# A transformer block pair on one core: a delta rule without GpSimd, deferred transposes, shared raw buffers and single-step weight sums

## The chip, the cores and the metric

The kernel runs on one core of a Trainium2 chip. The core has TensorE (matrix products, "PE"), VectorE ("DVE"), ScalarE ("ACT"), GpSimd ("POOL") and SyncE ("SP", which here only issues DMA transfers). Each takes its instructions in the order in which they were written for it, and they wait for each other by semaphores. The metric is the device time of one execution in microseconds.

## The reference

Two blocks work on 512 tokens of width 1024, in float32. All of this is computed:

- Block one: `x + mixer(rmsnorm(x))`. The mixer projects to seven groups of columns; one half is a spatial gating in chunks of 128, the other a gated delta rule with 4 heads of 128 (state `S_t = exp(g)(I − beta k kᵀ) S_{t−1} + beta k vᵀ`, output `Sᵀq`, normalised and gated); both go through `w_out`. Then cross-attention on a memory of 256 rows (`xa_wq`, `xa_wk`, `xa_wv`, `xa_wo`), then `square(relu(h @ ffn_w1)) @ ffn_w2` with 4096 hidden columns.
- Block two: a mixer of an mLSTM (4 heads) and a sliding-window attention (16 heads), two gates, two branch products and `w_out_2`; an MLP of the same shape (`w_up`, `w_down`); a gated product with a per-layer embedding; a last norm.

## The kernel before

Activations lie with features on the partitions: 8 tiles of 128x512. To hold float32 precision every operand is split into a rounded part and a rest, and every product is three matmuls (`mm3`, L285–L287: hi·hi, hi·lo, lo·hi into one PSUM tile). A weight granule of 128x8x256 (512 KB) is loaded by SyncE into a raw buffer `wr` (L263), cast to `wh` by ScalarE (L266), and the rest `wl = wr − wh` is made by VectorE (L267). So each granule passes SyncE's queue, ScalarE's queue and VectorE's queue before TensorE can use it, and the next load needs a raw buffer that L267 has released.

The order of instructions on each engine is set by a scheduler over the written program, which also moves later products ahead to fill TensorE; `keep_in_program_order` and `issue_after` add edges that it must hold.

Stages by time: projections and spatial gating 0–75 us; delta rule 75–310; rest of `w_out` and cross-attention to 395; first MLP to 800; second mixer to 1180; gates, branches, `w_out_2` to 1340; second MLP to 1700; the last product to the end.

**Delta rule.** `dn_head` handles one head with 128x128 tiles, 4 at a time (one PSUM bank, tag `c0` or `c1` by the head's parity, two buffers each). It transposes q, k, v (L565), takes their norms (`rsqrt` by small integer and Newton steps, L180–L185, on VectorE), makes the decay mask `E` (`slg`: L594 on GpSimd, L571 on TensorE, exp L597 on ScalarE, mask L598 on GpSimd, scale L599 on VectorE), `ked`, `kdec`, `vt` (L601, L602, L610), `M` and `QKT` (L605, L608), three masked copies of `M` (L626, GpSimd), inverts the triangular part by 15 steps of L642/L644 and block products (L622–L682), and scans the chunks (L696 `dY`, L702 `dS`, L709 and L713 `do`). At the end `o` is multiplied with the gate (L727, GpSimd) and with its norm (L728, VectorE), transposed on TensorE (L731) and split (L317/L318) for `w_out`. TensorE fills a head's waits with other products: `do_qk`, `do_v` (projections of later heads), `do_wa` (`w_out`'s first half), and `memory()` (L768, the memory's k and v).

**MLPs.** The second product of each MLP is done by seven products in place of eight of half-size blocks. Besides blocks a11, a12, a21, a22 of a weight it needs four sums of them. `sum_jobs` makes sums in DRAM by DMA: copies issued by ScalarE (L217) and accumulating copies issued by GpSimd (L220). `job()` is called at each weight granule and, every third or second call, runs one step. For `ffn_w2` two of the four sums are made so, and the third and fourth by one VectorE addition of 128x1024 (L890) into a raw buffer of its own; `w_down_2` has all four made by DMA, 1 MB of copies and 1 MB of adds per step, all in the second mixer and after. `st_weights` loads them (L887), splits them (L314/L315); `st_gemm` runs the seven products into PSUM tiles X, Y, Z and adds them to the residual (L924). In the MLPs raw, hi and lo buffers rotate together: three sets, or two "x" sets, of which two and two raw.

**Second mixer.** L1187 (mLSTM mask on VectorE) feeds L1197; L1263/L1264 split a query for the attention's scores L1285. The gate granules `w_in_ga` are read between.

## Time and profile before

| | |
|---|---|
| time, median of 3 | 1746.3 us (1746.27 to 1752.83) |
| profiled execution | 1746.58 us, span 1744.8 us |
| busy in the span | PE 97%, DVE 70%, ACT 46%, POOL 8% |
| bytes by DMA | 226.62 MB, mean 130 GB/s |

Windows are stretches of the span: busy time of each engine in it, instructions in brackets, then the granted TensorE clock (1.00 is full), the mean busy share of the 16 DMA engines and GB/s. A row of waits has the engine, its line, what it waited for, total us, times, the longest. A timeline row has start and duration in us, engine, line, operation, tiles, and in square brackets how long the engine was idle before and what ended it. A group's row has count, busy us and mean ns.

### The profile page before, as it was taken

The page shows a single profiled execution, that of the slowest core. Times are in us where ns is not written, and L with a number is a line of the kernel's source. Part 1 is how long each engine was busy: PE and PEld are TensorE (multiplying, and loading weights), DVE is VectorE, ACT ScalarE, POOL GpSimd, SP SyncE. Part 2 cuts the span into 40 slices and gives each one's busy share as a digit, 9 for nine tenths or more (in the row PEclk, how much of TensorE's full clock was granted, in tenths as well). Part 3 has the DMA queues.
Part 4 walks back from the last instruction along what each step waited for, and adds up shares of the span by engine and source line. Part 5 has one row for each costly group of instructions (what it writes and reads, how often), then busy time and mean ns, then how long its engine had stood idle before and what let it go on. Part 6 is the DMA issues. An engine that isn't in the chain of part 4 may idle for free.

```text
span 1744.8 us, 26033 instructions
## 1 busy us (share of the span) xinstructions
PE 1694.7 (97%) x9924; PEld 1465.6 (84%) x9924; DVE 1222.6 (70%) x2532; ACT 800.3 (46%) x1386; POOL 137.6 (8%) x156
## 2 busy tenths in 40 slices
PE   9999999999999999999999999999999999999998
PEld 8987788777898989888888886777888888898987
DVE  6998886756686777679745568775566766666775
ACT  5344544444444343444444456653244444444553
POOL 2212111100101000000010201011100000000000
PEclk9999999999999999999999999999999999999999
DMA  6322244716648353324477845449772343444331
GB/s 198 98 74 63 66 119 117 169 60 184 155 134 216 98 175 111 131 85 120 103 164 175 182 98 101 118 111 232 159 204 79 127 151 118 147 128 141 115 121 49
DMA packets 88605, 226.62 MB, mean 130 GB/s; under 512 B 13600, under 2 KB 14752, under 8 KB 88480
## 3 DMA queue, kind: packets, MB, share of 16 engines
q1 hardware_dynamic: 60368, 173.48, 31.1%
q0 software_dynamic: 13824, 25.17, 10.4%
q10 hardware_dynamic: 14288, 26.30, 5.5%
q8 instruction: 78, 1.28, 0.3%
q14 instruction: 47, 0.39, 0.1%
HBM read 222.56 MB, written 52.43 MB: 158 GB/s over the span
## 4 chain that ended last, share of the span: by engine, by line
PE 77%; DVE 11%; DMA 6%; ACT 4%; issue 2%; SPq 0%; ACTq 0%; DVEq 0%
PE psd L286 19%; PE psd L287 19%; PE psd L285 19%; PE x L285 4%; PE x L286 3%; PE x L287 3%; DVE wl L267 2%; ACT wh L266 1%; DMA wr<-in_w_in_ga_dram 1%; PE c L622 1%; PE lg L1285 1%; DMA wr<-sums_ffn_w 1%; PE po L1312 1%; DVE e L372 1%; ACT wh L314 1%
## 5 line engine op out<-in xcount | busy, mean ns | idle before, releaser
L285 PE MATMUL psd<-S,wh 128*128 128x512 f32 (+1 forms) x1256 | 484.2, 386 | 2.6 <-DVE e L768 1.7
L287 PE MATMUL psd<-S,wl 128*128 128x512 f32 (+1 forms) x1256 | 484.8, 387 | 0.8 <-DVE wl L267 0.8
L286 PE MATMUL psd<-S,wh 128*128 128x512 f32 (+1 forms) x1192 | 458.8, 385 | 0.5 <-DVE S L315 0.5
L267 DVE TENSOR_TENSOR wl<-wr,wh 128x1024 fp32r<-128x1024 f32 (+3 forms) x190 | 229.8, 1210 | 144.9 <-ACT wh L266 143.8
L266 ACT CAST wh<-wr 128x1024 fp32r<-128x1024 f32 (+3 forms) x190 | 194.6, 1025 | 214.4 <-PE psd L286 93.0
L285 PEld LDWEIGHTS psd<-S,wh 128*128 128x128 f32 x1256 | 237.3, 189 | 48.7 <-DVE e L768 1.9
L287 PEld LDWEIGHTS psd<-S,wl 128*128 128x128 f32 x1256 | 236.6, 189 | 46.2 <-DVE wl L267 1.6
L286 PEld LDWEIGHTS psd<-S,wh 128*128 128x128 f32 x1192 | 225.2, 189 | 43.3 <-DVE S L315 1.2
L285 PE MATMUL psd<-wh,S 128*128 128x256 f32 (+2 forms) x480 | 136.1, 284 | 1.2 <-ACT S L1090 1.2
L286 PE MATMUL psd<-wl,S 128*128 128x256 f32 (+2 forms) x480 | 136.4, 284 | 0.7 <-DVE wl L267 0.7
L287 PE MATMUL psd<-wh,S 128*128 128x256 f32 (+2 forms) x480 | 136.1, 284 | 0.0
L285 PE MATMUL x<-S,wh 128*128 128x256 f32 x452 | 129.0, 287 | 3.5 <-DVE x_fm L924 2.5
L286 PE MATMUL x<-S,wh 128*128 128x256 f32 x452 | 126.6, 281 | 0.0
L287 PE MATMUL x<-S,wl 128*128 128x256 f32 x452 | 125.8, 281 | 0.0
L314 ACT CAST wh<-wr 128x1024 fp32r<-128x1024 f32 (+1 forms) x76 | 71.5, 942 | 118.4 <-PE psd L286 40.1
L924 DVE TENSOR_TENSOR x_fm<-x_fm,x 128x256 f32<-128x256 f32 x192 | 78.7, 418 | 45.8 <-PE x L287 45.3
L286 PE MATMUL psd<-S,whx 128*128 128x512 f32 (+1 forms) x296 | 108.5, 366 | 0.0
L285 PE MATMUL psd<-S,whx 128*128 128x512 f32 (+1 forms) x296 | 108.0, 366 | 0.0
L287 PE MATMUL psd<-S,wlx 128*128 128x512 f32 (+1 forms) x296 | 107.2, 362 | 0.0
L315 DVE TENSOR_TENSOR wl<-wr,wh 128x1024 fp32r<-128x1024 f32 (+1 forms) x76 | 82.7, 1090 | 28.3 <-ACT wh L314 27.5
L285 PE MATMUL x<-S,whx 128*128 128x256 f32 x316 | 91.5, 290 | 5.1 <-DVE x_fm L924 2.5
L285 PEld LDWEIGHTS psd<-wh,S 128*128 128x128 f32 x480 | 91.0, 190 | 1.8 <-ACT S L1090 1.4
(460 smaller groups left out, 3198.3 us busy)
## 6 DMA issues: line engine op xcount, KB each, us to landing
wr<-in_ffn_w_dram SPq DMA_DIRECT2D x30, 512.0 KB
wr<-in_w_up_dram SPq DMA_DIRECT2D x20, 512.0 KB
wrx<-in_ffn_w_dram SPq DMA_DIRECT2D x18, 512.0 KB
wr<-sums_w_down SPq DMA_DIRECT2D x18, 512.0 KB
wr<-in_w_in_qk_dram SPq DMA_DIRECT2D x16, 512.0 KB
sums_ffn_w<-in_ffn_w_dram ACTq DMA_DIRECT2D x32, 256.0 KB
sums_w_down<-in_w_down_dram ACTq DMA_DIRECT2D x16, 512.0 KB
sums_w_down<-in_w_down_dram ACTq DMA_DIRECT2D x32, 256.0 KB
```

What stands on the lines that cost most here:

```text
L266: nc.scalar.copy(hi[:, c], raw[:, c])
L267: nc.vector.tensor_tensor(out=lo[:, c], in0=raw[:, c], in1=hi[:, c].bitcast(F32), op=ALU.subtract)
L285: mm(ps, ah, bh, start=first, stop=False, skip_group_check=more)
L286: mm(ps, ah, bl, start=False, stop=False, skip_group_check=more)
L287: mm(ps, al, bh, start=False, stop=last, skip_group_check=more)
L314: nc.scalar.copy(hi, src)
L315: nc.vector.tensor_tensor(out=lo, in0=src, in1=hi.bitcast(F32), op=ALU.subtract)
L372: nc.vector.scalar_tensor_tensor(out=c[:, s:], in0=xr[:, :T - s], scalar=w(j), in1=c[:, s:], op0=ALU.mult, op1=ALU.add)
L622: nc.tensor.matmul(ps[:, b * n:(b + 1) * n], lhs[:, b], rhs(b), start=True, stop=True)
L924: TT(out=x[n][t], in0=x[n][t], in1=ps, op=op)
L1285: nc.tensor.matmul(ps[:, i, K0:], qs[:, 2 * e2 + i, cs], kd[:, w, kc], start=(w == 0), stop=(w == 1))
L1312: nc.tensor.matmul(po, vhl[:, kb, j], pT[:, w], start=(kk == kks[0] and w == 0), stop=(kk == 1 and w == 1))
```

## The change

1. In `dn_head` GpSimd does nothing more. `slg` is four ScalarE copies with a scale (L602 in the new numbering); mask and scale of `E` are four VectorE operations in place of one on each of two engines; `ked`, `kdec`, `vt` are four, three and four ScalarE copies (L609) in place of VectorE operations; masked copies, memsets and the gate (L736) go to VectorE; the scale by the norm goes to ScalarE (four times L738). The sum of squares in the mixer's norm goes from GpSimd to VectorE.
2. A head's last step (transposes, now L743, and split) is returned as `fin` and written later, behind the last matmul written by then. `do_wa` 0 to 3 and `do_qk(3)` stand before head 3, `memory()` is a generator whose eight granules are written around and after head 3.
3. In the MLPs raw buffers rotate by themselves, five in all, and the third and fourth sums are computed into a11/a12's own raw buffer.
4. Both MLPs have two sums made by DMA and two by VectorE. A job is one 256 KB copy or one 256 KB add; all jobs of both are queued during the first mixer, two are run per granule up to the first MLP, then one, and one more in each `st_gemm`.
5. The seven products come in another order (a12 second).

Three places of the order. The first is the end of head 1's solve on TensorE. `c_…` are PSUM tiles, dV, dS, dY and vt belong to head 1 here, dk and dq to head 2. Before:

```order
L676 MATMUL c_297_1768<-dT_1669,dM_1654 64x64 x4
L286 MATMUL psd_2733<-S_122_933,wh_2714 128x512
L287 MATMUL psd_2733<-S_121_932,wl_2715 128x512
L285 MATMUL psd_2733<-S_121_932,wh_2714 128x512
L681 MATMUL c_299_1775<-dV_1679,dA_298_1773 64x64 x4
```

and now (L676 and L681 are L685 and L690):

```order
L690 MATMUL c_298_1797<-dV_1701,dA_297_1795 64x64 x4
L578 MATMUL c_392_2248<-dk_1890 128x128 x3
L578 MATMUL c_299_1803<-vt_1660,dV_1701 128x128 x4
L578 MATMUL c_300_1809<-dV_1701,ked_1659 128x128 x4
L578 MATMUL c_394_2255<-dq_1889,dk_1890 128x128
L711 MATMUL c_302_1816<-vt_1660,kdec_1658 128x128
L578 MATMUL c_394_2255<-dq_1889,dk_1890 128x128 x3
L718 MATMUL c_304_1820<-vt_1660,QKT_1680 128x128
L705 MATMUL c_305_1823<-dS_303_1818,ked_1659 128x128
L572 MATMUL c_396_2262<-masks,dv_1973 128x128 x4
```

Head 2's products L578 into c_392 and c_394 stand among head 1's last steps, and large projections no longer part them. VectorE at the same place, now:

```order
L691 TENSOR_TENSOR dV_1701<-dV_1701,c_298_1797 64x4x64
L593 TENSOR_TENSOR ds_384_2216<-ds_384_2216,beta_1058 128x4
L597 TENSOR_TENSOR dvi_2221<-dss_2182,dry_2203 128x4
L730 TENSOR_SCALAR dsc_2444<-dry_2203 128x4
L595 TENSOR_TENSOR dkd_2219<-ds_384_2216,ee_1093 128x4
L607 SCALAR_TENSOR_TENSOR slg_2223<-slg_2223,ds_384_2216,masks 128x128 x4
L308 SCALAR_TENSOR_TENSOR S_459_2572<-e_464_2586,vec,S_458_2571 128x256
L614 TENSOR_TENSOR dM_2253<-c_392_2248,slg_2223 128x512
```

Head 2's L595 (dkd, which L609 needs for kdec) stands behind head 1's L691, which waits for L690; the copies of kdec release the PSUM buffer into which c_394 goes.

The second place is VectorE's end of head 3, from the second Newton step on. Before:

```order
L185 SCALAR_TENSOR_TENSOR doy_2690<-dot_2691,doy_2690 128x4
L318 SCALAR_TENSOR_TENSOR S_595_3188<-psd_3430,rsmy_2880,S_594_3187 128x256
L183 TENSOR_TENSOR dot_2691<-doy_2690 128x4
L267 TENSOR_TENSOR wl_3557<-wr_3555,wh_3556 128x1024
L184 SCALAR_TENSOR_TENSOR dot_2691<-dot_2691,dso_2678 128x4
```

and now:

```order
L184 SCALAR_TENSOR_TENSOR doy_3002<-dot_3003,doy_3002 128x4
L182 TENSOR_TENSOR dot_3003<-doy_3002 128x4
L183 SCALAR_TENSOR_TENSOR dot_3003<-dot_3003,dso_2990 128x4
L184 SCALAR_TENSOR_TENSOR doy_3002<-dot_3003,doy_3002 128x4
L735 TENSOR_TENSOR dsc_2996<-dsc_2996,doy_3002 128x4
```

The steps of other work between are gone. On TensorE, the matmuls between the head's last L713 (now L722) and its transposes were 28 of 256 and 17 of 512 columns and are now 15 of 512 columns.

The third place is GpSimd's queue of the `w_down` sums. Before:

```order
L220 DMA sums_w_down_2_81<-in_w_down_dram 128x512 x2
L220 DMA sums_w_down_1_80<-sums_w_down_1_80 128x512
L220 DMA sums_w_down_0_79<-sums_w_down_0_79 128x512
L220 DMA sums_w_down_3_82<-in_w_down_dram 128x512 x2
L220 DMA sums_w_down_2_81<-sums_w_down_2_81 128x512
```

and now:

```order
L222 DMA sums_w_down_0_79<-in_w_down_dram 128x512
L222 DMA sums_w_down_0_79<-sums_w_down_0_79 128x512
L222 DMA sums_w_down_1_80<-in_w_down_dram 128x512
L222 DMA sums_w_down_1_80<-sums_w_down_1_80 128x512
L222 DMA sums_w_down_2_81<-in_w_down_dram 128x512
```

Four adds per group became two, one in each job. The diff, cut to its core:

```diff
-        self.sums = {n: [self.dp.tile([P, m, T], F32, tag=f"{n}{g}", name=f"sums_{n}_{g}") for g in range(16)]
-                     for n, m in (("ffn_w2", 2), ("w_down_2", 4))}
-        self.jobs, self.calls, self.every = [], 0, 1
-        self.adder = tc.nc.gpsimd
+        self.sums = {n: [self.dp.tile([P, 2, T], F32, tag=f"{n}{g}", name=f"sums_{n}_{g}") for g in range(16)]
+                     for n in ("ffn_w2", "w_down_2")}
+        self.jobs, self.made, self.rate, self.rn = [], {}, 1, 0
...
-        full = S[0].shape[1] == 4
-        def copy(o, i):
-            self.tc.keep_in_program_order(nc.scalar.dma_start(o, i))
-        def add(o, i):
-            self.tc.keep_in_program_order(nc.gpsimd.dma_start(o, i, accum_op=ALU.add))
-        def step(i):
-            if i < n:
-                a, s = W[i], S[i]
-                copy(s[:, 1::2], a[:, 0:s.shape[1] // 2])
-                for j in range(0, s.shape[1], 2):
-                    copy(s[:, j:j + 1], a[:, 2:3])
-            if 0 <= i - 1 < n:
-                a, s = W[i - 1], S[i - 1]
-                add(s[:, 0:1], a[:, 3:4])
-                if full:
-                    add(s[:, 2:3], a[:, 0:1])
-            if 0 <= i - 2 < n:
-                s = S[i - 2]
-                add(s[:, 1:2], s[:, 0:1])
-            if full and 0 <= i - 3 < n:
-                s = S[i - 3]
-                add(s[:, 3:4], s[:, 1:2])
-        self.jobs += [(lambda i=i: step(i)) for i in range(n + 2 + full)]
+        self.made[name] = 0
+        def copy(i, j, k):
+            if 0 <= i < n:
+                with self.tc.issue_after(self.last_cast.ins):
+                    nc.scalar.dma_start(S[i][:, j:j + 1], W[i][:, k:k + 1])
+        def add(i, j, src):
+            if 0 <= i < n:
+                nc.gpsimd.dma_start(S[i][:, j:j + 1], src(i), accum_op=ALU.add)
+                self.made[name] += j
+        for i in range(n + 2):
+            self.jobs += [lambda i=i: copy(i, 0, 2), lambda i=i: add(i - 1, 0, lambda g: W[g][:, 3:4]),
+                          lambda i=i: copy(i, 1, 0), lambda i=i: add(i - 2, 1, lambda g: S[g][:, 0:1])]
     def job(self):
-        self.calls += 1
-        if self.jobs and self.calls % self.every == 0:
-            self.jobs.pop(0)()
+        for _ in range(self.rate):
+            if self.jobs:
+                self.jobs.pop(0)()
     def wtiles(self, kt, n):
-        p, b, x = self.wp, (2, 3), ""
+        p, b, x = self.wp, 3, ""
+        q, c, y = self.wp, 2, ""
         if self.wx is not None:
-            self.wn = (self.wn + 1) % 5
+            self.wn, self.rn = (self.wn + 1) % 5, (self.rn + 1) % 5
             if self.wn > 2:
-                p, b, x = self.wx, (2, 2), "x"
-        return (self.t(p, [P, kt, n], "wr" + x, bufs=b[0]), self.t(p, [P, kt, n], "wh" + x, F32R, bufs=b[1]),
-                self.t(p, [P, kt, n], "wl" + x, F32R, bufs=b[1]))
+                p, b, x = self.wx, 2, "x"
+            if self.rn > 1:
+                q, c, y = self.wx, 3, "x"
+        return (lambda: self.t(q, [P, kt, n], "wr" + y, bufs=c), lambda: self.t(p, [P, kt, n], "wh" + x, F32R, bufs=b),
+                lambda: self.t(p, [P, kt, n], "wl" + x, F32R, bufs=b))
...
-            eng = self.adder if k < KT - 1 else nc.vector
-            eng.tensor_tensor(out=acc, in0=acc, in1=sq, op=ALU.add)
+            nc.vector.tensor_tensor(out=acc, in0=acc, in1=sq, op=ALU.add)
...
-            self.dn_head(h, *qk[h], v[h], pr, gate, yb_h, yb_l)
+            fins.append(self.dn_head(h, *qk[h], v[h], pr, gate, yb_h, yb_l))
...
         do_head(1)
         do_qk(2)
         do_v(2)
-        do_head(2)
         do_wa(0)
         do_qk(3)
+        self.behind(fins[0])
+        do_head(2)
+        for g in (1, 2, 3):
+            do_wa(g)
+        self.sum_jobs("ffn_w2")
+        self.sum_jobs("w_down_2")
+        self.rate = 2
+        next(mem)
+        self.behind(fins[1])
         do_head(3)
-        do_wa(1)
-        do_wa(2)
-        do_wa(3)
+        for _ in range(5):
+            next(mem)
+        self.behind(fins[2])
+        next(mem)
+        next(mem)
+        fins[3]()
         self.yb = ([yb_h[:, k] for k in range(4)], [yb_l[:, k] for k in range(4)])
+    def behind(self, f):
+        with self.tc.issue_after(self.last_mm.ins):
+            f()
...
-        nc.gpsimd.tensor_tensor(out=slg, in0=self.maskb("slower"), in1=pr["g"][:, :, h:h + 1].broadcast_to([P, NB, P]), op=ALU.mult)
+        for b in range(NB):
+            nc.scalar.activation(slg[:, b], self.mask("slower"), AF.Copy, scale=pr["g"][:, b, h:h + 1])
         psD = mm4(lambda b: slg[:, b], lambda b: self.mask("upper"))
         E = slg
         nc.scalar.activation(E, v4(psD), AF.Exp)
-        nc.gpsimd.tensor_tensor(out=E, in0=E, in1=self.maskb("upper"), op=ALU.mult)
-        TT(out=E, in0=E, in1=col(s1), op=ALU.mult)
+        for b in range(NB):
+            V.scalar_tensor_tensor(out=E[:, b], in0=E[:, b], scalar=s1[:, b:b + 1], in1=self.mask("upper"), op0=ALU.mult, op1=ALU.mult)
         kdec, ked, vt = b4("kdec"), b4("ked"), b4("vt")
-        TT(out=ked, in0=v4(psk), in1=ed.broadcast_to([P, NB, P]), op=ALU.mult)
-        TT(out=kdec[:, :NB - 1], in0=v4(psk)[:, :NB - 1], in1=col(kd)[:, :NB - 1], op=ALU.mult)
+        scaled = lambda out, ps, f, n=NB: [nc.scalar.activation(out[:, b], blk(ps, b), AF.Copy, scale=f(b)) for b in range(n)]
+        scaled(ked, psk, lambda b: ed[:, b])
+        scaled(kdec, psk, lambda b: kd[:, b:b + 1], NB - 1)
...
-        TT(out=vt, in0=v4(psv), in1=col(ri), op=ALU.mult)
+        scaled(vt, psv, lambda b: ri[:, b:b + 1])
...
-            nc.gpsimd.tensor_tensor(out=out, in0=M, in1=self.maskb(n), op=ALU.mult)
+            TT(out=out, in0=M, in1=self.maskb(n), op=ALU.mult)
...
-        nc.gpsimd.memset(Tb, 0.0)
-        nc.gpsimd.memset(flat(Tb)[:, 0::17], 1.0)
+        V.memset(Tb, 0.0)
+        V.memset(flat(Tb)[:, 0::17], 1.0)
...
-        nc.gpsimd.tensor_tensor(out=o, in0=o, in1=gate[:, :, h * P:(h + 1) * P], op=ALU.mult)
-        TT(out=o, in0=o, in1=col(sc), op=ALU.mult)
-        psy = psc()
+        TT(out=o, in0=o, in1=gate[:, :, h * P:(h + 1) * P], op=ALU.mult)
         for b in range(NB):
-            nc.tensor.transpose(blk(psy, b), o[:, b], ident)
-        self.split_sb(yb_h[:, h], yb_l[:, h], psy, self.vec[:, C_ONORM:C_ONORM + 1])
+            nc.scalar.activation(o[:, b], o[:, b], AF.Copy, scale=sc[:, b:b + 1])
+        def fin():
+            psy = psc()
+            for b in range(NB):
+                nc.tensor.transpose(blk(psy, b), o[:, b], ident)
+            self.split_sb(yb_h[:, h], yb_l[:, h], psy, self.vec[:, C_ONORM:C_ONORM + 1])
+        return fin
...
+        while self.made[name] <= g:
+            self.jobs.pop(0)()
...
+        def parts_of(raw):
+            rn = self.rn
+            _, hi, lo = self.wtiles(2, T)
+            self.rn = rn
+            return raw, hi(), lo()
+        def load(*srcs):
+            raw, hi, lo = (f() for f in self.wtiles(2, T))
             j = 0
             for src in srcs:
                 m = src.shape[1]
                 nc.sync.dma_start(raw[:, j:j + m], src)
                 j += m
-            if not srcs:
-                nc.vector.tensor_tensor(out=raw, in0=ra, in1=rb, op=ALU.add)
-            c = slice(first, first + n)
+            return raw, hi, lo
+        def split(raw, hi, lo, c=slice(0, 2)):
             self.split_sb(hi[:, c], lo[:, c], raw[:, c])
-            out.extend((hi[:, i], lo[:, i]) for i in range(first, first + n))
-            return raw
-        ra = part([a[:, 0:2]])
-        if s.shape[1] == 4:
-            part([s[:, 0:2]])
-            part([s[:, 2:4]])
-            part([a[:, 3:4]], 1)
-            return [out[i] for i in (0, 2, 3, 1, 4, 5, 6)]
-        part([s[:, 0:1], a[:, 3:4]])
-        rb = part([a[:, 2:3], s[:, 1:2]], 1, 1)
-        part([])
-        return [out[i] for i in (0, 2, 4, 1, 5, 6, 3)]
+            return [(hi[:, i], lo[:, i]) for i in range(c.start, c.stop)]
+        A = load(a[:, 0:2])
+        a11, a12 = split(*A)
+        B = load(a[:, 2:3], s[:, 1:2])
+        s2, = split(*B, slice(1, 2))
+        C = load(s[:, 0:1], a[:, 3:4])
+        nc.vector.tensor_tensor(out=A[0], in0=A[0], in1=B[0], op=ALU.add)
+        s1, a22 = split(*C)
+        s3, s4 = split(*parts_of(A[0]))
+        return a11, a12, s2, s1, s3, s4, a22
...
         w = self.st_weights(name, g)
+        self.job()
...
-        prod(1, Z, 4, True)
-        add(1, 1, Z, ALU.subtract)
+        prod(1, Y, 1, True)
+        add(0, 0, Y)
         prod(2, X, 5, False)
         add(0, 1, X)
-        prod(3, Y, 1, True)
-        add(0, 0, Y)
+        prod(3, Z, 4, True)
+        add(1, 1, Z, ALU.subtract)
...
-        K.mixer()
-        K.adder = K.nc.vector
-        K.sum_jobs("ffn_w2")
-        K.every = 3
-        mem = K.memory()
+        mem = K.mixer()
...
-        K.every = 1
+        K.rate = 1
...
-        K.sum_jobs("w_down_2")
-        K.every = 2
```

20 lines of the change are left out of this document (11 added, 9 removed).

## The prediction

> **What bounds the kernel now.** I read busy time by stage first, then the waits of TensorE in each stage, the granted clock around the longest of them, and last the instructions there.
>
> ```profile
> core 0: us, PE busy (x) PEld busy (x) DVE busy (x) ACT busy (x) POOL busy (x), PEclk, DMA share, GB/s
> 425.00:450.00 25.00, 25.00 (x109) 20.29 (x108) 12.91 (x16) 8.98 (x12) 4.14 (x5) 1.00 0.66 166
> 75.00:310.00 235.00, 222.42 (x1473) 195.47 (x1472) 199.18 (x535) 107.77 (x261) 37.55 (x33) 0.99 0.32 93
> 400.00:800.00 400.00, 393.43 (x2333) 345.81 (x2332) 288.42 (x454) 181.05 (x245) 17.33 (x21) 1.00 0.49 141
> 800.00:1180.00 380.00, 364.67 (x2130) 310.33 (x2129) 260.00 (x715) 192.53 (x411) 37.67 (x45) 0.98 0.56 131
> 1340.00:1700.00 360.00, 356.30 (x2179) 315.29 (x2178) 250.66 (x412) 165.89 (x228) 0.00 (x0) 1.00 0.40 129
> ```
>
> TensorE bounds it. Where it runs without a gap (109 matmuls of 512 columns in 25 us, 229 ns each) nothing can be had, and the change keeps the number of matmuls. What can move is the time in which TensorE is idle, length less busy time: 12.6 us in the delta rule (75–310), 6.6 in the first MLP (400–800), 15.3 in the second mixer (800–1180), 3.7 in the second MLP (1340–1700). The waits of these four stretches, in that order:
>
> ```profile
> PE c L731 <- DVE do L728: 6.6, 4, 2.4
> PE c L571 <- DVE kdec L602: 1.8, 2, 1.1
> PE psd L285 <- DVE e L768: 1.7, 1, 1.7
> PE c L622 <- DVE dTb L648: 1.3, 2, 1.0
> ...
> PE x L285 <- ACT whx L314: 3.3, 3, 2.2
> PE x L285 <- DVE x_fm L924: 2.1, 4, 0.9
> ...
> PE lg L1285 <- DVE qs L1264: 5.0, 3, 4.2
> PE m L1197 <- DVE E L1187: 3.1, 1, 3.1
> ...
> PE x L285 <- DVE x_fm L924: 3.0, 4, 1.4
> ```
>
> A long wait costs more than itself, since the granted clock falls behind it:
>
> ```profile
> 180.00:184.00 4.00, 3.63 (x16) 3.34 (x17) 3.96 (x8) 1.85 (x6) 0.00 (x0) 0.59 0.00 0
> 768.00:772.00 4.00, 4.00 (x23) 4.00 (x23) 2.75 (x4) 0.62 (x1) 0.00 (x0) 0.60 0.34 119
> 884.00:888.00 4.00, 2.90 (x14) 2.46 (x15) 4.00 (x10) 0.96 (x2) 3.30 (x4) 1.00 0.83 183
> 1096.00:1100.00 4.00, 0.21 (x1) 0.00 (x0) 1.52 (x2) 2.20 (x3) 0.00 (x0) 0.86 0.70 202
> 1100.00:1104.00 4.00, 3.55 (x14) 3.34 (x14) 3.46 (x8) 1.62 (x2) 0.00 (x0) 0.50 0.46 136
> 1104.00:1108.00 4.00, 4.00 (x19) 3.38 (x19) 2.58 (x18) 2.12 (x9) 0.00 (x0) 0.78 0.44 131
> ```
>
> Lost clock is (1 − PEclk) × 4 us: 1.6 behind the L731 wait at 180, 1.6 behind the whx wait, 3.4 (0.6 + 2.0 + 0.9) around the L1285 wait. Behind the L1197 wait at 885 nothing was lost, so it isn't certain.
>
> **Part 1, the engines of a delta head.** GpSimd's work goes away, and that matters through VectorE:
>
> ```profile
> 230.40 1.28 POOL L598 TENSOR_TENSOR slg<-slg,masks 128x512 f32<-128x512 f32 x1 [17.44 <-ACT slg L597]
> 232.19 1.26 POOL L626 TENSOR_TENSOR dA<-dM,masks 128x512 f32<-128x512 f32 x1 [0.51 <-DVE dry L185]
> 230.50 1.22 DVE L644 TENSOR_TENSOR dV<-dV,dA 32x28 f32<-32x28 f32 x1
> 232.23 1.24 DVE L183 TENSOR_TENSOR drt<-dry 128x8 f32<-128x8 f32 x1
> L648 DVE TENSOR_TENSOR dTb<-dY,masks 128x128 f32<-128x128 f32 x4 | 3.2, 796 | 0.2 <-DMA dY<-dV 0.2
> ```
>
> A VectorE operation that starts within a GpSimd one ends with it: 128x8 takes 1.24 us, 32x28 1.22. The 1.7 us wait for e L768 stands at 234.07, right behind these two holds, and dTb's 796 ns is such a hold as well (1.3 us of waits). I count both as gained, **+3.0**. The wait for kdec (1.8) I leave: its chain at 115 us is VectorE's square-root steps, which stay.
>
> What VectorE gets in return:
>
> ```profile
> L599 DVE TENSOR_TENSOR slg<-slg,ds 128x512 f32<-128x512 f32 x4 | 2.7, 683 | 0.0
> L707 DVE SCALAR_TENSOR_TENSOR dS<-dS,ee,c 128x128 f32<-128x128 f32 x8 | 2.8, 345 | 1.0 <-PE c L702 0.9
> L719 ACT ACTIVATE dA<-do 128x128 f32<-128x128 f32 x16 | 4.9, 308 | 5.2 <-DVE do L715 5.2
> L685 ACT COPY vt<-c 128x512 f32<-128x512 f32 x4 | 2.3, 585 | 4.3 <-PE c L571 4.3
> ```
>
> By the 683 ns of 128x512 it gives up L599, L601, L610, L728 and three quarters of that for L602 (about 3.2 us a head) and takes three masks, the gate (4 × 0.68) and four mask-and-scale steps (4 × 0.345), 4.1 us: +0.9 a head, against holds of about 1 us each at five GpSimd operations a head. ScalarE gets 19 operations of about 308 ns, 5.9 us a head; it is busy 107.8 of 235 us and covers them on average. Where the cover is gone it shows as the collision in part 3.
>
> **Part 2, the deferred transposes.** Two of the four L731 waits, those of the first and the last head:
>
> ```profile
> 180.37 0.81 PE L731 MATMUL c<-masks,do 128*128 128x128 f32 x4 [2.04 <-DVE do L728]
> 306.94 0.63 PE L731 MATMUL c<-masks,do 128*128 128x128 f32 x4 [1.49 <-DVE do L728]
> ```
>
> The longest, 2.4, is head 2's, and 0.7 is left for head 1. From the order of both programs, TensorE's work between a head's last L713/L722 and its transposes, counted at 229 ns per 512-column matmul and half that for 256, goes from 6.6 to 10.7 us (head 0), 11.2 to 12.7, 9.0 to 10.8, and 7.5 to 3.6 (head 3). Heads 0 and 1 then don't wait, head 2 about 0.6. Head 3, whose place is shown in the order, loses 3.9 us of cover; its chain (about 8.9 us: 7.5 of cover and 1.5 of wait) loses the two weight subtractions and two smaller steps that stood within it (about 2.5 us, by the 1.23 of L267 below), so it needs 6.4 and waits 2.8. Waits go from 6.6 to 3.4: **+3.2**. The 1.6 us of clock at 180 comes back, I take as much behind head 2's longer wait, and one such loss appears behind head 3: **+1.6**.
>
> **Part 3, what is late next.** The order shows the end of head 1 (L690, L711, L718, L705) between the first products of head 2. There head 2's L578 into c_394 needs ScalarE's L609 (three × 308), which needs the fourth small VectorE step behind L691, which needs L690, just ahead on TensorE. By the rows: 0.4 + 0.8 + 0.9 us against eight small matmuls of about 1 us and their own wait, 1 us short in all; then L711 waits for the copy of vt (585, behind one ScalarE step of 0.5) 0.9, L718 for the next copy 0.7, and the scan's three L711/L705 pairs about 0.3 each, since their VectorE steps stand behind masks of 0.68. **−3.4**. Head 2 against head 3 has less of it, **−1**. Delta stage: 3.0 + 3.2 + 1.6 − 3.4 − 1 = +3.4; from +15 (all 11.4 of its waits and the clock, no collision) to −5 (collision doubled with a clock loss each, no fin gain).
>
> **Part 4, the sums by DMA.** In the second mixer a step of w_down's sums is 1 MB of copies and 1 MB of adds at once:
>
> ```profile
> 870.40 0.33 SPq L263 DMA_DIRECT2D wr<-in_w_in_ga_dram  x1
> 881.71 1.05 ACT L266 CAST wh<-wr 128x1024 fp32r<-128x1024 f32 x1 [4.51 <-DMA wr<-in_w_in_ga_dram]
> 882.78 1.23 DVE L267 TENSOR_TENSOR wl<-wr,wh 128x1024 fp32r<-128x1024 f32 x1 [7.12 <-ACT wh L266]
> 883.92 1.12 DVE L1187 TENSOR_SCALAR E<-m,c 128x128 f32<-128x128 f32 x4
> 885.10 0.55 PE L1197 MATMUL m<-masks,mk 128*128 128x128 f32 x3 [3.12 <-DVE E L1187]
> 1097.37 1.04 ACT L266 CAST wh<-wr 128x1024 fp32r<-128x1024 f32 x1 [4.61 <-DMA wr<-in_w_in_ga_dram]
> sums_w_down<-sums_w_down POOLq DMA_DIRECT2D x4, 256.0 KB, 9.5
> ```
>
> A 512 KB weight load lands 11 us after its issue, ScalarE's cast holds its queue 4.5 us, VectorE waits for it with L1187 queued behind, and TensorE waits for that. The same again before 1100. With one 256 KB step per weight granule, a quarter of the bytes, the loads should land in time: 3.1 + 4.2 + 3.4 of clock = 10.7 at best, 3 if only one goes; I take **+9**.
>
> In the first MLP the raw buffers count where a cast came late. Of the 3.3 us behind whx the longest, 2.2, follows six ScalarE steps of the residual, not a load. **+2**, from 0 to 7.
>
> The second MLP becomes what the first one is: sums three and four by one 1.22 us VectorE addition (L890) in each of 16 groups, 19.5 us on top of 250.7 of 360. The first MLP, which runs so already, waits 3.6 us more on whx and wh than the second; with five raw buffers I take **−1.5**, from 0 to −4.4 with a clock loss. Product order and the loads' fewer bytes I cost at nothing: TensorE reads the same operands, and DMA share there is 0.40.
>
> ```profile
> L890 DVE TENSOR_TENSOR wr<-wrx,wr 128x1024 f32<-128x1024 f32 x6 | 7.3, 1222 | 0.1
> ```
>
> **Sum.** 3.4 + 2 + 9 − 1.5 = 12.9. The profiled execution took 1746.58 us (span 1744.8), 0.3 above the median of 1746.3: 1733.7, or 1733.4 on the median.
>
> **A rule against the clock terms.** The sum counts 1.6 us of clock in the delta stage and most of 3.4 in the second mixer as following from waits. The Trainium skill ("TensorE: Matmul & The Clock Gate", Part 1: The HAM clock gate) has the clock halve only when TensorE idles through a free-running window of about 3.4 us; by it the waits of 2.0 to 2.4 us should cost no clock. The trace shows 0.59 behind a wait of 2.04 us and 1.00 behind one of 3.12, so it bears the rule out at the second place alone. By the rule the sum would be 1.6 less and the time 1735.0.
>
> **Rivals.**
> A. The relief in the second mixer doesn't come: the cast there waits for a load in any case, as SyncE issues in order and two w_in_o loads stand beside it. For it: casts also wait for w_br loads at 1185–1235, where they cost nothing. Then +9 is +1 and the sum 4.9: about 1741.5.
> B. All goes: no collision, no wait left at head 3, both stalls with their clock: delta +11, MLP +5, mixer +10.7: about 1719.
> C. The clock losses have another cause than these waits and stay: minus 1.6 and about 2.5, 1737.5.
> D. Slower: the sums now run before the first MLP at two steps per granule, 0.5 MB, from head 3 on, where up to now they were a third of a MB. If a load there is held as at 870–881, the cast of 4.5 us stands in ScalarE's queue ahead of the delta heads' copies, at 3.1 to 4.2 us plus up to 3.4 of clock a time. At about 6.5 each, four such places cost 26: 1759. It turns the sign from the third on. Against it: in 310–400 TensorE lost nothing to loads, and the old mixer rate was twice this one.
>
> **How the numbers follow.** 0.5% (8.7 us) is about what a measurement of this kernel can tell from no change; faster means under 1737.6. My case 0.42 (its own range 1727–1738), A 0.20, B 0.16, C 0.10, D 0.12 (of which a third ends within 0.5%). Faster: 0.40 + 0.16 + 0.06 and a little of A, 0.64; slower 0.09; same 0.27. The range 1718 to 1746 takes in B's time and A; D's slower half and all beyond B are left out.
>
> **What would show it.** L743 (the old L731) waits under 1 us in heads 0–2 and 2 to 4 at head 3; L183 and L644 never 1.2 us in the delta stage; waits of 0.3–1 us at L578/L711/L718 between heads 1 and 2; no cast waiting 4 us on w_in_ga with L1197 or L1308 (the old L1285) behind it; PEclk 1.00 at 1100; x_fm and whx waits of the second MLP like the first one's. I am wrong if casts still wait for w_in_ga, if the delta stage is longer than 235 us, or if the second MLP loses over 4.

## The result: 1706.7 us, and where it went

The changed kernel takes 1706.68 us (median of 4 runs, 1706.09 to 1707.82) against 1749.57 for the kernel before, measured beside it: a ratio of 0.975, 95% interval 0.973 to 0.978. That is 42.9 us less where the prediction had 12.9, and outside its range. The two profiled executions, on which the stages below are read, differ by 38.8 us.

Busy time by stage of the changed kernel (delta rule, first MLP, second mixer, second MLP; columns as in the prediction's first fence):

```profile
75.00:300.00 225.00, 218.99 (x1471) 193.66 (x1470) 183.01 (x546) 126.86 (x337) 9.88 (x12) 0.99 0.44 114
388.00:780.00 392.00, 389.64 (x2331) 342.58 (x2330) 284.51 (x454) 179.05 (x246) 12.19 (x15) 1.00 0.48 136
780.00:1145.00 365.00, 361.16 (x2138) 307.48 (x2137) 260.25 (x718) 196.43 (x417) 10.57 (x13) 1.00 0.34 92
1300.00:1663.00 363.00, 361.19 (x2211) 319.88 (x2210) 268.98 (x440) 168.66 (x231) 8.99 (x11) 1.00 0.45 132
```

TensorE's idle time, length less busy time, was 12.6, 6.6, 15.3 and 3.7 us in these stages and is 6.0, 2.4, 3.8 and 1.8. Its waits, in the same order of stages:

```profile
PE c L743 <- ACT do L738: 1.8, 1, 1.8
PE c L578 <- ACT c L587: 1.7, 2, 1.5
PE c L631 <- DVE dTb L657: 1.0, 1, 1.0
PE psd L275 <- ACT S L307: 0.8, 1, 0.8
...
PE x L275 <- DVE x_fm L947: 2.0, 2, 1.7
...
PE lg L1308 <- DVE qs L1287: 0.7, 2, 0.4
...
PE x L275 <- DVE x_fm L947: 0.9, 1, 0.9
```

The long waits of the attention (L1285, now L1308) and of the mLSTM are gone, the MLPs keep one or two short ones, and the delta rule has a few of 1 to 2 us, of which head 3's transposes (L743) are the longest.

Besides idle time there is time lost to the clock, (1 − PEclk) × length summed over 4 us windows: before 3.4, 1.7, 6.8 and 0.0 us, now 3.4, 0.0, 0.0 and 0.0.

To compare stages of two kernels whose ends lie at different times, I added up TensorE's work (each matmul at its duration without hindrance) and compared the times at which both had done the same amount. Gain over the profiled execution of before, in us. The rows add up to 0.2 to 2.7 us less than the spans differ by (the gates with their branches and the last product have no column), so 2 us is nothing:

| | start | delta rule, cross-att. | first MLP | second mixer | second MLP | median, us |
|---|---|---|---|---|---|---|
| predicted | 0 | 3.4 | 2 | 9 | −1.5 | 1733.5 |
| changed kernel | 1.8 | 8.3 | 7.6 | 16.8 | 3.5 | 1706.7 |
| b_twosums | 0.7 | 0.6 | −0.6 | 16.9 | −3.3 | 1732.0 |
| b_small2 | −0.2 | −1.4 | 1.3 | 17.2 | −4.3 | 1733.8 |
| a_four | 1.3 | 9.5 | 8.3 | −3.6 | 4.2 | 1729.3 |
| a_burst | 1.4 | 7.8 | 7.6 | 16.5 | 3.7 | 1707.2 |
| a_ctl | 1.7 | 2.9 | 7.4 | 15.7 | 4.0 | 1708.7 |
| a_plain | 2.6 | −0.7 | 7.6 | 11.7 | 3.8 | 1717.9 |
| a_acc | 0.7 | 10.7 | 7.8 | 10.5 | 3.7 | 1713.5 |
| b_raw | −0.8 | −0.4 | 8.6 | −2.0 | 4.1 | 1735.0 |
| a_raw4 | 1.2 | 4.7 | −0.6 | 15.8 | −2.2 | 1724.7 |
| a_order | 2.0 | 4.1 | 8.7 | 17.0 | 4.1 | 1706.0 |
| b_engines | 2.4 | −10.3 | 0.2 | 1.7 | −4.5 | 1757.9 |
| a_gpsimd | 0.9 | −4.4 | 7.6 | 15.7 | 4.2 | 1719.4 |
| a_finnow | 1.8 | 0.5 | 7.5 | 15.0 | 3.9 | 1713.1 |
| a_mem | 0.8 | 3.5 | 7.6 | 16.6 | 4.0 | 1711.3 |
| v_headfirst | 2.5 | 5.9 | 8.2 | 16.8 | 3.8 | 1715.5 |

A name with b_ is the kernel before with one part of the change, one with a_ or v_ the changed kernel with one part undone or altered. The medians of before beside them were 1748.5 to 1751.6.

### The profile page after: what moved, and what is told of

Read it like the earlier page. It is cut to its first block, busy times and chain, and to the rows that moved or that the text cites. A ratio compares the mean times of both kernels' runs of the same rounds, so it can differ in the third digit from the quotient of the medians.

```text
span 1706.0 us, 25979 instructions
## 1 busy us (share of the span) xinstructions
PE 1681.1 (99%) x9924; PEld 1456.4 (85%) x9924; DVE 1216.6 (71%) x2574; ACT 822.0 (48%) x1462; POOL 66.3 (4%) x86
## 4 chain that ended last, share of the span: by engine, by line
PE 88%; DVE 7%; ACT 2%; issue 1%; DMA 1%; SPq 0%; ACTq 0%; DVEq 0%
PE psd L276 21%; PE psd L275 21%; PE psd L277 21%; PE x L275 5%; PE x L276 5%; PE x L277 5%; DVE wl L257 1%; PE c L578 1%; PE c L631 1%; PE lg L1308 1%; PE po L1335 1%; ACT wh L256 1%; DVE acc L318 1%; DVE S L418 1%; PE m L1229 1%
## 5 line engine op out<-in xcount | busy, mean ns | idle before, releaser
L257 DVE TENSOR_TENSOR wl<-wr,wh 128x1024 fp32r<-128x1024 f32 (+2 forms) x160 | 192.0, 1200 | 107.6 <-ACT wh L256 107.0
L256 ACT CAST wh<-wr 128x1024 fp32r<-128x1024 f32 (+2 forms) x160 | 164.0, 1026 | 160.3 <-PE psd L276 112.3
L276 PEld LDWEIGHTS psd<-wl,S 128*128 128x128 f32 x480 | 90.4, 188 | 1.0 <-DVE wl L257 0.5
L275 PEld LDWEIGHTS psd<-wh,S 128*128 128x128 f32 x480 | 90.3, 188 | 0.4
L277 PEld LDWEIGHTS psd<-wh,S 128*128 128x128 f32 x480 | 90.5, 188 | 0.0
L275 PEld LDWEIGHTS x<-S,wh 128*128 128x128 f32 x452 | 84.9, 188 | 6.1 <-DVE x_fm L947 2.9
```

The source lines that it names most:

```text
L256: self.last_cast = nc.scalar.copy(hi[:, c], raw[:, c])
L257: nc.vector.tensor_tensor(out=lo[:, c], in0=raw[:, c], in1=hi[:, c].bitcast(F32), op=ALU.subtract)
L275: mm(ps, ah, bh, start=first, stop=False, skip_group_check=more)
L276: mm(ps, ah, bl, start=False, stop=False, skip_group_check=more)
L277: self.last_mm = mm(ps, al, bh, start=False, stop=last, skip_group_check=more)
```

## The experiments

### The second mixer: bytes, steps, or another order

Theory: w_down's sums moved too many bytes in this stage, loads of weights came late, and casts behind them held the attention. Rivals: the grain of the steps (how many transfers are issued at once) did it, or the order of instructions, which the scheduler writes anew when the transfers change.

**b_twosums**: two sums by DMA only, in before's steps.

```diff
-   for n, m in (("ffn_w2", 2), ("w_down_2", 4))}
+   for n, m in (("ffn_w2", 2), ("w_down_2", 2))}
```

> The kernel before, with two of w_down's four sums by DMA (a step is 0.5 MB of copies and 0.5 MB of adds, still issued together on every second granule) and the other two by one VectorE addition, as ffn_w2 has them. Theory bytes: the second mixer's 15.7 us came from the halved DMA traffic; then most of it comes here too, 10 us or more, less 2 us in the second MLP: 1738 us or under. Rival grain: it came from single steps; then a burst of half the size still holds the cast of w_in_ga, the gain in the mixer is under 5 and the time within 3 us of before.

Ratio to before 0.989 (0.987 to 0.991). The second mixer gains all of its 16.9 us from this number alone; the second MLP loses 3.3.

**a_four**: the changed kernel with four sums of w_down in before's steps.

```diff
-        self.sum_jobs("w_down_2")          # in the first mixer
+        K.step_jobs("w_down_2")            # before's step(i), in the second mixer, every second granule
```

> The changed kernel, with all four sums of w_down by DMA again in the old steps (1 MB of copies, 1 MB of adds on every second granule of the second mixer and after); ffn_w2's sums stay single steps. If the sums alone made the second mixer's gain, 12 to 15 us come back there: 1719 to 1722. If the rest of the change (order, GpSimd) made part of the attention chain's gain, less than 8. The second MLP, without its 16 additions on VectorE, shows whether they cost anything: up to 2 us faster there, if so.

0.987 (0.985 to 0.989): the 16.8 us are gone, and before's waits are back. TensorE's waits in the second mixer of this run:

```profile
PE lg L1350 <- DVE qs L1329: 5.8, 3, 5.1
PE m L1262 <- DVE E L1252: 3.2, 1, 3.2
PE pt L1372 <- DVE lg L1366: 2.8, 3, 2.5
```

and who waited for the loads of in_w_in_ga (engine, line, us, times):

```profile
  ACT wh L294: 11.0, 3
```

**a_burst**: the changed kernel's own jobs, eight at every eighth granule of the second mixer.

```diff
+        k = 0 if self.calls % 8 else 8     # in place of one job at each granule
```

> The changed kernel, with the same jobs and bytes, but in the second mixer and its branches eight jobs (four copies and four adds of 256 KB) are issued together at every eighth granule. Theory grain: casts of w_in_ga wait 4 us again where a burst falls, TensorE waits 3 us at each of two or three places, and the clock falls behind: 1713 to 1720. Theory bytes: mean traffic is the same, so within 2 us of the change, 1706 to 1709.

0.975 (0.973 to 0.977), the changed kernel's time. The grain is worth nothing at these bytes.

**b_small2**: before, with the transfers of w_down's sums cut to 64 of 512 columns. The sums are then not made; the second MLP loads blocks of w_down in their place, so that its product leaves the sums out.

```diff
+   nc.gpsimd.dma_start(o[..., :64], i[..., :64], accum_op=ALU.add)   # the copies likewise
-   part([s[:, 0:2]])
+   part([a[:, 0:2]])
```

> The kernel before, with every copy and add of w_down's four sums issued as before, but on 64 of 512 columns: the same number of transfers and issues with an eighth of the bytes. The second MLP loads blocks of w_down itself in place of the sums (so the sums are left out of the product). Theory bytes: the second mixer gains what it did with two sums, 13 to 16 us, and the second MLP loses nothing: 1733 to 1737. Rival issues: the time is in the number of issues on ScalarE's and GpSimd's queues; then under 4 us.

0.991 (0.988 to 0.995). With all issues and an eighth of the bytes the second mixer gains 17.2: not the issues, the bytes. The second MLP loses 4.3 here, with loads of the same size, at one place: a wait of 2.46 us for x_fm at 1482 us and 1.7 us of clock behind it. b_engines, whose second MLP is not changed at all, loses 4.5 there in the same way (2.70 us at 1506, and the clock). What makes x_fm late there stays open.

But in all of these the scheduler had also written another order on TensorE, since it plans with the bytes. The same place of the attention, its seventh group of transposes, in TensorE's timeline of before and of the changed kernel:

```profile
1077.37 0.86 PE L1312 MATMUL po<-pT,S 128*128 128x512 f32 x3
1080.72 0.30 PE L1307 MATMUL pt<-masks,lg 128*128 128x128 f32 x1 [2.50 <-DVE lg L1301]
```

```profile
1053.27 0.39 PE L1335 MATMUL po<-pT,S 128*128 128x512 f32 x1
1056.74 0.27 PE L1330 MATMUL pt<-masks,lg 128*128 128x128 f32 x1
```

Before, the transposes follow the value products at once and wait 2.50 us for VectorE; now 14 large products stand in the 3.5 us between, and nothing waits. a_four, with before's bytes back, has before's row of products at this place again, and its wait of 2.50 us. So six runs were made to part order and bytes.

**a_extra1, a_extra2, a_extraacc**: the changed kernel with copies that nobody reads, issued by GpSimd at every second granule of the second mixer; TensorE's, VectorE's and ScalarE's order stays row for row.

```diff
+        for j in range(4):   # a_extra1; a_extra2 a second such loop, a_extraacc a second one with accum_op
+            self.nc.gpsimd.dma_start(scr[i][:, j:j + 1], W[i][:, j:j + 1])
```

> The changed kernel with 1 MB of copies that nobody reads (four of 256 KB from w_down to a scratch buffer in DRAM, issued by GpSimd) at every second weight granule of the second mixer. The order of the instructions on TensorE, VectorE and ScalarE is that of the changed kernel, row for row. Theory 1, the bytes in flight cost the time while the program runs: half of before's bytes come back, so the second mixer loses 3 to 9 us of its 15.7, and loads of w_in_ga land some 7 us after their issue. Theory 2, the order of the instructions costs it (with fewer bytes the scheduler writes another order, with 14 other matmuls between the attention's products where before had none): nothing is lost, 1707 within 2 us.

> The same with 2 MB of plain copies at every second granule, as many transfers as before had. Theory 1: the second mixer loses 8 to 19 us, 1715 to 1726, with a cast 4 us late at w_in_ga and TensorE waiting at L1197 or L1308. Theory 2: under 2 us lost, the same order with the transfers landing late but covered.

> The same with 1 MB of plain copies and 1 MB of accumulating copies at every second granule, before's kinds and bytes. Theory 1: the second mixer loses 8 to 19 us (1715 to 1726), more than with plain copies if the accumulation is what costs. Theory 2: under 2 us, and then before's 15.7 us are the order's.

These missed the question. Nothing held the copies, GpSimd's queue is empty now, and they moved from the program's start on. Ratios 0.992 (0.989 to 0.995), 1.008 (1.004 to 1.011) and 1.019 (1.014 to 1.024): at the start, where TensorE lives on its first loads, they cost 26, 58 and 81 us by the end of the delta rule, and nothing after. The first 100 us of the changed kernel, of a_extra2 and of a_extraacc:

```profile
0.00:100.00 100.00, 96.55 (x610) 87.26 (x611) 82.06 (x201) 49.53 (x80) 14.10 (x22) 1.00 0.43 134
```

```profile
0.00:100.00 100.00, 83.31 (x495) 72.04 (x496) 61.70 (x159) 38.36 (x60) 49.32 (x90) 0.97 0.88 278
```

```profile
0.00:100.00 100.00, 80.78 (x423) 69.35 (x424) 48.29 (x136) 33.04 (x52) 46.80 (x72) 0.86 1.01 246
```

**a_ctl, a_plain, a_acc**: a small copy issued by ScalarE in its order marks every second granule (a_ctl); behind each marker GpSimd issues three copies and three more (a_plain), or three copies and three accumulating ones (a_acc), so that the kernel moves in this stage what before moved. TensorE's order differs from the changed kernel's in ten products ahead of the attention, SyncE's not at all.

```diff
+        with self.tc.issue_after(self.last_cast.ins):
+            self.nc.scalar.dma_start(scr[0][i][..., :8], W[i][..., :8])
+        for j in range(3): self.nc.gpsimd.dma_start(scr[0][i][:, j:j + 1], W[i][:, j:j + 1])
+        for j in range(3): self.nc.gpsimd.dma_start(scr[1][i][:, j:j + 1], scr[0][i][:, j:j + 1])   # a_acc: scr[0] from W, accum_op
```

> The changed kernel with one small copy (16 KB, into a scratch buffer that nobody reads) issued by ScalarE at every second weight granule of the second mixer, 19 in all; it is the marker by which the next two runs hold their transfers back to that stage, as their predecessors ran ahead to the start of the program. All theories: 1707 within 3 us; what it costs is taken off the next two.

> The same, and GpSimd issues six 256 KB copies behind each marker (three from w_down into the scratch buffer, three on into another), so that with the kernel's own sums 2 MB move per two granules, as before the change. The order on TensorE is that of the changed kernel but for ten matmuls ahead of the attention; SyncE's is the same. Theory 1, transfers in flight: the second mixer loses 8 to 19 us against the run with the markers, with casts late at w_in_ga. Theory 2, the scheduler's order: under 3 us lost.

> The same with three copies and three accumulating copies behind each marker, before's kinds of transfer. Theory 1: 8 to 19 us lost in the second mixer, more than with copies alone if accumulation is the heavier kind (its median from issue to landing was 11.1 us against 8.2 us for a copy in the runs that ran ahead). Theory 2: under 3 us.

0.974 (0.971 to 0.977), 0.979 (0.976 to 0.982) and 0.978 (0.975 to 0.981). The bytes are there: DMA share of the second mixer in a_plain and a_acc, before's being 0.56:

```profile
800.00:1180.00 380.00, 373.37 (x2168) 317.02 (x2168) 265.31 (x707) 206.15 (x432) 51.79 (x91) 0.99 0.52 143
```

```profile
800.00:1180.00 380.00, 376.44 (x2176) 318.82 (x2175) 264.97 (x699) 204.05 (x429) 64.75 (x91) 1.00 0.62 144
```

and they cost 4.0 and 5.2 us of a_ctl's 15.7, all of it at the stage's entry, where ScalarE waits for a load and TensorE behind it. ScalarE's row and TensorE's row of a_acc:

```profile
ACT wh L267 <- DMA wr<-in_w_in_v_dram: 4.9, 1, 4.9
...
PE pss L349 <- DVE e L346: 3.5, 1, 3.5
```

In a_plain and a_acc no cast waits for w_in_ga (in a_ctl one does, for 2.1 us), and from the entry on to the end of the stage the three runs gain 15.4, 16.3 and 14.6 us over before. So neither theory holds alone. Transfers in flight can cost about 5 us in this stage, but at its entry, where before waited hardly more than the changed kernel (2.6 and 1.6 us). With as many transfers as before had, all of before's long waits stay away in the new order of the instructions, which is another because the bytes were fewer when it was written.

That it is the order alone is not shown. Before, the two loads of w_in_ga that came late met a DMA share of 0.95 and 0.83 in the 12 us from their issue (870.4 and 1088.2); the same two loads of a_acc (852.3 and 1049.9) met 0.42 and 0.44, those of a_plain 0.29 and 0.15, so the added transfers missed them. What speaks for the order is the room that it leaves them: before, ScalarE was ready for the cast 6.8 and 4.6 us after the issue and had it 11.3 and 9.2 us after, while in a_acc the casts come 11.5 and 15.6 us after the issue and wait for no load. By these numbers even a load as late as before's would hold almost nothing there (an estimate, no run has it). Which rule of the scheduler makes the order wasn't looked into, and before's order with the changed kernel's bytes wasn't tried.

### The MLPs: raw buffers

Theory: five raw buffers that rotate by themselves make the gain. Rival: the order of the products and of their loads.

**b_raw**: before with the five raw buffers and the sums made in place. **a_raw4**: the changed kernel with four. **a_order**: the changed kernel with before's order of products and loads.

```diff
-            self.wn = (self.wn + 1) % 5
+            self.wn, self.rn = (self.wn + 1) % 5, (self.rn + 1) % 5     # b_raw; a_raw4 has (self.rn + 1) % 4
```

```diff
-        return a11, a12, s2, s1, s3, s4, a22     # a_order, with the products and loads to match
+        return a11, s1, s2, a12, s3, s4, a22
```

> The kernel before, with raw buffers that rotate by themselves in the MLPs (five, the third and fourth sums computed in a11/a12's raw buffer); product order, sums by DMA and delta heads as before. At equal work done the change gained 7.6 us in the first MLP and 3.3 in the second. Theory raw: loads start earlier and casts stop being late, so 5 us or more of the 7.6 come here, 1 to 2 in the second MLP: 1738 to 1741. Rival order: the waits behind x_fm and whx went because of the order of products; then under 2 us in the first MLP.

> The changed kernel with four raw buffers in the MLPs, not five (as many as before the change; they still rotate by themselves, and the third and fourth sums use a11/a12's own). Theory number: the fifth buffer is what lets the loads run ahead, so half or more of the MLPs' 11 us come back, 1711 to 1717. Rival rotation: that the sum takes no buffer and that raw and split buffers are released apart is enough, within 2 us of the change.

> The changed kernel, with the seven products and their loads in the old order (s1 second, a12 fourth). Theory raw: nothing, 1706 to 1709. Rival order: the two MLPs lose 5 to 10 us together, with waits for x_fm and whx as before: 1712 to 1717.

b_raw 0.992 (0.989 to 0.995), with 8.6 and 4.1 us gained in the MLPs; a_raw4 0.986 (0.982 to 0.989), with both gains gone; a_order 0.974 (0.970 to 0.978), no different from the changed kernel. It is the fifth buffer. TensorE's waits in the first MLP of a_raw4; in b_raw no row of an x tile is left in either MLP:

```profile
PE x L275 <- DVE x_fm L947: 8.6, 10, 1.7
```

### The delta rule

Theory: GpSimd's holds on VectorE and the waits for the transposes. Rivals: each part of the change brings its gain alone, or they only work together.

**b_engines**: before with the new engines only. **a_gpsimd**: the changed kernel with the old engines in the heads. **a_finnow**: each head's transposes written at once. **a_mem**: before's places of do_wa, do_qk and memory(). **v_headfirst**: do_wa 1 to 3 behind head 3.

```diff
-        nc.gpsimd.tensor_tensor(out=o, in0=o, in1=gate[:, :, h * P:(h + 1) * P], op=ALU.mult)   # b_engines; a_gpsimd the reverse
+        TT(out=o, in0=o, in1=gate[:, :, h * P:(h + 1) * P], op=ALU.mult)
```

```diff
-            fins.append(self.dn_head(h, *qk[h], v[h], pr, gate, yb_h, yb_l))      # a_finnow
+            self.dn_head(h, *qk[h], v[h], pr, gate, yb_h, yb_l)()
```

```diff
+        do_head(2); do_wa(0); do_qk(3)                  # a_mem
+        do_head(3); do_wa(1); do_wa(2); do_wa(3)
```

```diff
-        for g in (1, 2, 3): do_wa(g)                    # v_headfirst: now behind do_head(3)
```

> The kernel before, with only the engines of a delta head changed (GpSimd's work to ScalarE and VectorE, the four copies with a scale, sums of squares to VectorE); transposes, order of the program, raw buffers and sums as before. My sum had 3.0 us for the holds that vanish: 1743. The trace after shows 8.3 us gained in the delta stage and 1.8 ahead of it, with the deferral losing about 5 at head 3: if the engines carry that, 1734 to 1738. If the chains of a head get longer by the four small operations each, no gain.

> The changed kernel, with a delta head's work on GpSimd and VectorE as before (masks, decay mask, gate, scaled copies); the deferral, the program order, sums and buffers as changed. With only the engines changed in the kernel before, the heads up to the third were 12 us ahead at equal work. So without them here: 8 to 12 us back, 1714 to 1719, with VectorE operations of 1.2 us under each GpSimd one. If the interleaving hides the chains in any case, under 3.

> The changed kernel, with each head's transposes and split written right after the head, as before; engines, order of do_wa, do_qk and memory, sums and buffers as changed. My step: heads 0 to 2 wait 2.0, 0.7 and 2.4 us again and lose about 3 of clock, head 3 stays as it is: 1711 to 1715. If the shorter chains on VectorE already had the transposes in time, within 2 us of the change.

> The changed kernel, with the old program order of the delta stage (do_wa(0) and do_qk(3) behind head 2, the other do_wa and the whole memory behind head 3), transposes still deferred. With the changed engines in the kernel before, TensorE ran ahead to head 3 and then waited 3.2, 2.3 and 5.2 us for its chain with the clock down. Theory order: the order of the products is what saves that, so 10 us or more come back, 1716 to 1722. Rival deferral: deferring the transposes was enough, 1707 to 1711.

> The changed kernel, with do_wa 1 to 3 written behind head 3 in place of ahead of it. In the order of the program TensorE's work between head 3's last scan product and its transposes goes from 3.4 to 8.8 us (more than the 5.2 of the chain that is left there), for 22 in place of 10.7 at head 2. If head 3's chain sets the end of the delta stage, its wait of 1.8 us, the 0.8 behind it and the clock lost there go: 1701 to 1703. If other waits of head 3 take their place (the products are then missing earlier), 1705 to 1710.

b_engines 1.004 (1.002 to 1.006): 0.4% slower than before. Its TensorE ends head 1 8.6 us earlier (transposes at 213.3 us in place of 221.8) and has by then spent products that would fill the last heads:

```profile
PE c L623 <- DVE dTb L649: 5.5, 2, 3.2
PE c L733 <- ACT do L730: 5.2, 1, 5.2
```

a_gpsimd 0.982 (0.977 to 0.986), a_finnow 0.977 (0.972 to 0.982), a_mem 0.978 (0.974 to 0.981), v_headfirst 0.980 (0.976 to 0.986). Their medians are 12.7, 6.4, 4.6 and 8.8 us above the changed kernel's. For a_gpsimd that is clear: its four executions (1716.0 to 1724.6) lie above all of the changed kernel's and of a_order's on the same chip (1703.1 to 1708.9). For the other three the intervals overlap, and the stage's gain alone settles nothing, since it scatters: the changed kernel, a_burst, a_order, a_four, a_raw4, a_ctl, a_plain and a_acc have the same instructions in the same order up to head 3's transposes and gain 8.3, 7.8, 4.1, 9.5, 4.7, 2.9, −0.7 and 10.7 there, a median of 6.3.

TensorE's idle time in this stage, length less busy time between the same amounts of work, scatters less: 6.1 to 8.5 us in these eight. It was 12.7 before, and is 12.6 in b_engines, 12.5 in a_gpsimd, 10.7 in a_finnow, 8.6 in a_mem and 7.9 in v_headfirst. The windows of before, the changed kernel, b_engines, a_gpsimd and a_finnow, 1891 matmuls each:

```profile
75.00:395.00 320.00, 307.34 (x1891) 263.76 (x1890) 253.53 (x634) 147.76 (x333) 41.77 (x37) 0.99 0.36 97
73.10:385.00 311.90, 305.80 (x1891) 263.52 (x1890) 238.55 (x650) 168.45 (x409) 14.76 (x18) 0.99 0.43 112
72.20:402.20 330.00, 317.40 (x1891) 272.89 (x1890) 238.81 (x650) 168.23 (x409) 7.54 (x9) 0.95 0.35 95
73.90:399.00 325.10, 312.61 (x1891) 269.15 (x1890) 253.55 (x635) 147.45 (x333) 48.44 (x46) 0.97 0.42 108
72.90:392.30 319.40, 308.75 (x1891) 265.57 (x1890) 237.89 (x650) 168.68 (x409) 14.77 (x18) 0.98 0.42 109
```

So the parts work only together: the engines alone save no idle time (b_engines), the rest without the engines saves none either (a_gpsimd), and engines and places without the deferral save 2 of the 6.6 us (a_finnow); these are one profile each. b_engines is slower because it loses 17.1 us of clock where before lost 3.4. The places of do_wa, do_qk and memory() are not settled. v_headfirst was meant as a better version and isn't one; no run is faster than the changed kernel by more than the noise.

## The prediction, point by point

The sum had 12.9 us, and the columns of the table come to 38.0. The 25 us that it missed lie in the second mixer (7.8), the first MLP (5.6), the second MLP (5.0), the delta rule (4.9) and ahead of it (1.8).

- **GpSimd's holds (+3.0)**: the mechanism was right. dTb and the Newton step, in the groups of the changed kernel, take 283 ns in place of 796 and 162 in place of 244:

```profile
L182 DVE TENSOR_TENSOR drt<-dry 128x8 f32<-128x8 f32 x12 | 1.9, 162 | 0.3
L657 DVE TENSOR_TENSOR dTb<-dY,masks 128x128 f32<-128x128 f32 x4 | 1.1, 283 | 0.8 <-DMA dY<-dV 0.8
```

  The wait for e L768 (1.7) went as counted, and of dTb's 1.3 a wait of 1.0 stayed. The wait for kdec (1.8), which I had left standing, went too, to 0.2. As a term of its own the 3.0 fails: with this part alone TensorE's idle time stays at 12.6 us (b_engines).
- **Deferred transposes (+3.2)**: heads 0 to 2 wait no more, head 3 waits 1.8 where I had 2.8; from 6.6 to 1.8. **Clock (+1.6)**: nothing, it was 3.4 us before and is 3.4 in the profiled execution; as the same instructions lose 0.0 to 10.2 us of it in other executions, that is chance.
- **The collision between heads (−3.4, −1)**: it didn't come. TensorE is busy 25.00 of 25 us there (windows, then timeline):

```profile
175.00:200.00 25.00, 25.00 (x178) 22.01 (x177) 20.57 (x57) 18.95 (x64) 0.97 (x1) 1.00 0.38 97
```

```profile
192.29 1.06 PE L578 MATMUL c<-vt,dV 128*128 128x128 f32 x8
193.18 1.06 PE L578 MATMUL c<-dV,ked 128*128 128x128 f32 x8
```

  The step that failed is the cover: I counted the eight small products between L690 and c_394 as about 1 us. Each takes two records, and the two groups last 1.78 us from 192.29 to the next matmul at 194.07; three more products, into c_392, stand ahead of them and take 0.78. ScalarE's copies of kdec end at 193.24, 0.8 us before c_394's products begin.
- **Delta stage (+3.4)**: 8.3 in the profiled execution, with a median of 6.3 for the same instructions. Both lie within the bounds given (−5 to +15), in part by luck: the terms were off singly, as above, and the clock's share is chance.
- **Second mixer (+9, at best 10.7)**: 16.8. The late loads were there, and the two stalls went with their clock. Mis-sized was the bound: 3.1 + 4.2 + 3.4. It left out the waits of L1307 and L1312 (2.50 and 0.73 us) at 1080, behind which no late load stood, and of the lost clock it counted 3.4 of 6.8. The ground of the term, that fewer bytes let the loads land in time, is not borne out as it stands: with before's transfers back, in the new order, none of these waits returned (a_plain, a_acc). How much of the gain fewer bytes would bring without a new order stays open. Rival A is out.
- **First MLP (+2, from 0 to 7)**: 7.6. What failed is the reading of one wait: I took the longest for one of ScalarE's residual steps, which more buffers wouldn't help; with five buffers the waits for whx (3.3) are gone, and with them the 1.7 us of clock that the prediction showed behind them and did not count.
- **Second MLP (−1.5)**: +3.5, the wrong sign. The price of the scheme was right: b_twosums loses 3.3 with two sums and before's buffers, and its products into x wait 6.6 us in place of 3.0. The step that failed is the worth of the fifth buffer, which more than covers that price (b_raw +4.1): the first MLP's waits were taken as if they'd stay. With five buffers the sixteen additions cost nothing that can be told: a_four, without them, gains 4.2.
- **Sums**: the collision's terms add up to 3.5, not 3.4; the waits on whx and wh in which the two MLPs differ are 4.0 us (3.3 and 0.7), not 3.6; and the rule set against the clock terms would have taken the second mixer's clock out of the sum too, not the 1.6 us alone.
- **Product order at nothing**: right (a_order). **Rivals**: B, "all goes", had 1719 and came nearest, C and D are out. The range was too narrow since MLPs and mixer all ended beyond their own bounds at once.

## What to carry to other kernels

Where a scheduler plans with transfer bytes, a change of bytes is a change of order: look at the new order of every stage that the bytes touch, not only at the loads that come late. Price a change of buffers by the waits it can remove including their lost clock, not by one wait and its nearest cause. And a stage that is short of filling work can get slower when its chains get faster, as long as the fillers aren't moved to where the chain now is. Where the clock scatters, compare TensorE's idle time over the same work, beside the stage's time.
